# Rounding the first weight folds, keeping the conditions in PSUM and reordering the second norm in a two-layer backbone kernel

## The chip, the cores and the metric

The kernel runs on one core of a Trainium2 chip. The time is device microseconds of one execution. In profile rows PE is TensorE (matrix products), DVE VectorE, ACT ScalarE, POOL GpSimd, SP the queue that issues most DMAs. SBUF is the on-chip memory, PSUM the banks into which PE writes.

## The reference

Batch 1, 1024 latent tokens, 256 context tokens, width 1024, two layers. What matters here, cut from the code:

```python
shift, scale, gate = jnp.split(silu(c) @ mod_w[l] + mod_b[l], 3, axis=-1)
hx = modulate(rmsnorm(x, norm_g[l]), shift[:, None], scale[:, None])
# even layer: (and the same for the context tokens with silu(c_ctx))
z = h @ w_in                    # va, vg, ga, xb, gb
# conv branch from va, vg, ga; recurrent branch from xb, gb; then @ w_out
# odd layer:
z = h @ w_in; u, g = jnp.split(z, [2048], axis=-1)
d = multiscale_pool(u)          # four groups of 512 channels
y = jnp.einsum("bngi,gij->bngj", d, w_grp) * scale
out = (y * silu(g)) @ w_out
x = x + gate * out
```

## The kernel before

Nearly all products of the kernel run on numbers rounded for TensorE's quick float32 form. An operand is split in a high part (a cast on ACT) and a low part (source minus high part, on POOL or DVE), and a product is three matmuls: high by high, high by low, low by high. This is `split`. A plain float32 matmul needs no split but takes PE longer.

The odd layer's pooling is linear over tokens, so its group weights can be multiplied into its input weights beforehand. This is the fold: for each of four groups g and four steps kp, 128-row blocks of `wu[g, kp]` times `grp[g]`, two halves s, four chunks i, summed in PSUM, copied by ACT to an `fo` tile and stored to DRAM as `wfold[g]`. Much later the odd layer loads `wfold` as its weights (`wr_v`). In names like `fold_1_2_0` stand group, step and half.

The kernel has a first stage and then one long chain of products. In the first stage the inputs are loaded, the conditions silu(c) are spread over all partitions (`cL` for the latent tokens, `cC` for the context, in SBUF), and `modulation(k)` computes shift and scale as dots: DVE multiplies a 128x1024 tile `mod` with cL or cC and sums along the row (`junk`), then adds the bias (`m`, `a`, tiny instructions of 128x2). The squares of x are summed, PE adds them over partitions (`ms_x`), `rstd_cols` takes the root and spreads it; DVE scales x (`scaled` rows: `x<-x,a,ms_x`), and `h0h`, `h0l` are the high and low part of the modulated x. The folds of groups 0 and 1 run on PE beside this as plain float32 matmuls (`fold_whole`); `fold_some(n)` sets how many steps are written at a place. Then the first product, xb, begins.

The late stage is at the end of the even layer. `quad` computes one 2x2 block product with seven products of half-size operands (a, c, b are PSUM banks, `put` evicts them). The last `quad` of the output projection `woa` ends with products t3 and t4 into bank b. There the second norm follows: the squares of the new x1 are summed in `nacc` by ACT and DVE, PE's column matmuls (128x1) sum over partitions, ACT takes the root, DVE builds the diagonal `dg`, a matmul with ones spreads it (`ms_n`), and DVE scales x1. The folds of groups 2 and 3 run here, rounded (`fold`), to fill PE meanwhile. After them the odd layer's products start (qa_v).

Within an engine the instructions run in the order in which a scheduler put them, from the written order and priorities (`tc.high_priority`, `tc.issue_after`); across engines they wait by semaphores.

## Time and profile before

| | |
|---|---|
| runs | 1288.49, 1291.21, 1292.29 us; median 1291.21 |
| span of the profiled execution | 1287.8 us |
| PE busy | 1271.1 us (99%) |
| DVE busy | 1141.3 us (89%) |
| ACT busy | 640.6 us (50%) |
| POOL busy | 354.3 us (28%) |
| mean granted TensorE clock | 0.998 |

The time of the profiled execution itself is not given beside its span, which is 3.4 us less than the median of the runs. The busy shares are averages over stages: DVE, for instance, is busy 39.5 us of the 40 from 40 to 80 us, and 24.8 of the 40 from 740 to 780.

### The profile page before, as it was taken

The page shows a single profiled execution, that of the slowest core. Times are in us where ns is not written, and L with a number is a line of the kernel's source. Part 1 is how long each engine was busy: PE and PEld are TensorE (multiplying, and loading weights), DVE is VectorE, ACT ScalarE, POOL GpSimd, SP SyncE. Part 2 cuts the span into 40 slices and gives each one's busy share as a digit, 9 for nine tenths or more (in the row PEclk, how much of TensorE's full clock was granted, in tenths as well). Part 3 has the DMA queues.
Part 4 walks back from the last instruction along what each step waited for, and adds up shares of the span by engine and source line. Part 5 has one row for each costly group of instructions (what it writes and reads, how often), then busy time and mean ns, then how long its engine had stood idle before and what let it go on. Part 6 is the DMA issues. An engine that isn't in the chain of part 4 may idle for free.

```text
span 1287.8 us, 15841 instructions
## 1 busy us (share of the span) xinstructions
PE 1271.1 (99%) x5650; PEld 1027.5 (80%) x5650; DVE 1141.3 (89%) x1775; ACT 640.6 (50%) x941; POOL 354.3 (28%) x180
## 2 busy tenths in 40 slices
PE   8999999999999999999999999999999999999997
PEld 4468888888888888888887888888888888878886
DVE  7979999999999999988789667999999997887876
ACT  5343656666657623227426345834444444654543
POOL 3063655675558603443220023000000000000002
PEclk9999999999999999999999999999999999999999
DMA  9934111121212133543555356243333324777723
GB/s 371 358 114 157 58 41 63 44 74 42 66 41 90 50 115 107 168 147 113 172 174 192 127 185 203 87 155 127 110 132 131 123 96 157 245 247 258 296 83 131
DMA packets 83075, 181.87 MB, mean 141 GB/s; under 512 B 7858, under 2 KB 27826, under 8 KB 82996
## 3 DMA queue, kind: packets, MB, share of 16 engines
q1 hardware_dynamic: 74548, 176.67, 40.1%
q10 hardware_dynamic: 8448, 4.20, 1.1%
q8 instruction: 44, 0.72, 0.2%
q14 instruction: 35, 0.29, 0.1%
HBM read 136.79 MB, written 44.04 MB: 140 GB/s over the span
## 4 chain that ended last, share of the span: by engine, by line
PE 86%; DVE 6%; DMA 5%; ACT 1%; issue 1%; SPq 0%; POOL 0%; POOLq 0%; DVEq 0%; ACTq 0%
PE vg L510 7%; PE wob L510 7%; PE gb L510 7%; PE va L510 7%; PE xb L510 6%; PE g L510 4%; PE fold L285 3%; PE ga L510 2%; PE qb_v L1000 2%; PE qb_v L1001 2%; PE qb_v L998 2%; PE xbc L510 2%; PE qb_g L1000 2%; PE qb_g L1001 2%; PE qb_g L998 2%; DMA x<-xT 1%
## 5 line engine op out<-in xcount | busy, mean ns | idle before, releaser
L510 DVE SCALAR_TENSOR_TENSOR conv<-u,sm,conv 128x505 f32<-128x505 f32 (+6 forms) x224 | 153.9, 748 | 0.9
L1762 POOL TENSOR_TENSOR o<-x,rr 128x256 f32<-128x256 f32 (+1 forms) x10 | 9.4, 971 | 445.7 <-ACT rr L1698 443.8
L510 POOL TENSOR_TENSOR l<-l,l 128x1280 f32<-128x1280 f32 (+1 forms) x23 | 64.0, 2798 | 91.8 <-DVE l L510 65.5
L510 ACT ACTIVATE l<-g,sm 128x512 f32<-128x512 f32 (+1 forms) x96 | 58.7, 619 | 57.7 <-PE g L510 57.0
L285 PE MATMUL fold<-graw,wu 128*128 128x512 f32 x128 | 58.0, 614 | 2.3 <-DMA wu<-wu 2.3
L102 ACT CAST wq_g<-wr_g 128x512 fp32r<-128x512 f32 x48 | 28.3, 622 | 48.4 <-DVE wr_g L979 17.6
L285 PEld LDWEIGHTS fold<-graw,wu 128*128 128x128 f32 x128 | 25.1, 198 | 33.7 <-issue 32.7
L510 PE MATMUL vg<-h0h,wl_vg 128*128 128x512 f32 x128 | 50.0, 390 | 0.0
L510 PE MATMUL wob<-ybh,wh_wob 128*128 128x512 f32 x128 | 49.9, 390 | 0.0
L510 PE MATMUL vg<-h0h,wh_vg 128*128 128x512 f32 x128 | 49.8, 389 | 0.0
L510 PE MATMUL gb<-h0l,wh_gb 128*128 128x512 f32 x128 | 49.8, 389 | 0.0
L510 PE MATMUL gb<-h0h,wh_gb 128*128 128x512 f32 x128 | 49.8, 389 | 0.0
L510 PE MATMUL wob<-ybh,wl_wob 128*128 128x512 f32 x128 | 49.8, 389 | 0.0
L510 PE MATMUL vg<-h0l,wh_vg 128*128 128x512 f32 x128 | 49.8, 389 | 0.0
L510 PE MATMUL wob<-ybl,wh_wob 128*128 128x512 f32 x128 | 49.8, 389 | 0.0
L510 PE MATMUL va<-h0h,wh_va 128*128 128x512 f32 x128 | 49.8, 389 | 0.0
L510 PE MATMUL va<-h0l,wh_va 128*128 128x512 f32 x128 | 49.8, 389 | 0.0
L510 PE MATMUL va<-h0h,wl_va 128*128 128x512 f32 x128 | 49.8, 389 | 0.0
L510 PE MATMUL gb<-h0h,wl_gb 128*128 128x512 f32 x128 | 49.8, 389 | 0.0
L510 DVE TENSOR_TENSOR_SCAN l<-l,l 128x256 f32<-128x256 f32 (+1 forms) x32 | 48.7, 1521 | 1.1
L103 POOL TENSOR_TENSOR wl_wu<-wr_wu,wh_wu 128x1024 fp32r<-128x1024 f32 x8 | 19.2, 2417 | 106.9 <-ACT wh_wu L102 104.4
L510 POOL TENSOR_TENSOR l<-l,uc 128x1280 f32<-128x1280 f32 x16 | 48.1, 3032 | 0.0
(642 smaller groups left out, 4344.0 us busy)
## 6 DMA issues: line engine op xcount, KB each, us to landing
mod<-modT SPq DMA_DIRECT2D x20, 512.0 KB, 5.5
x_part<-xp SPq DMA_DIRECT2D x32, 256.0 KB, 3.1
mod<-modT SPq DMA_DIRECT2D x32, 256.0 KB, 3.1
wr_v<-wfold SPq DMA_DIRECT2D x16, 512.0 KB, 4.0
wr_g<-wg SPq DMA_DIRECT2D x16, 512.0 KB, 4.2
wr_wo<-wo SPq DMA_DIRECT2D x16, 512.0 KB, 4.6
y_b<-y SPq DMA_DIRECT2D x24, 256.0 KB, 3.4
y_t<-y SPq DMA_DIRECT2D x24, 256.0 KB, 2.9
```

Source lines behind the costliest of these rows:

```text
L102: return (nc.scalar.copy(hi, src), eng.tensor_tensor(out=lo, in0=src, in1=hi.bitcast(F32), op=sub))
L103: eng.tensor_tensor(out=lo, in0=src, in1=hi.bitcast(F32), op=sub))
L285: nc.tensor.matmul(ps, w[:, kc], gs[i], start=(i == 0), stop=(i == 3))
L510: last[eng] = f(*args, **kw)
L998: nc.tensor.matmul(ps, hi, xh[k], start=(first and k == 0), stop=False, skip_group_check=not first)
L1000: nc.tensor.matmul(ps, hi, xl[k], start=False, stop=False, skip_group_check=not first)
L1001: mm = nc.tensor.matmul(ps, lo, xh[k], start=False, stop=(k == KH - 1), skip_group_check=not first)
L1762: nc.gpsimd.tensor_tensor(out=outs[k // per][:, k % per], in0=x1[k][:, cols], in1=rr, op=mult)
```

## The change

Three things change.

1. `fold_whole` becomes `fold_early`. Only the very first step, (0,0), stays plain float32. The other steps of groups 0 and 1 are three rounded products, and two of the four steps of group 2 come into the first stage. The raw group weights and the weights of each step are split: casts on ACT, subtractions on POOL (one on DVE). Group 0's results are stored later (`fold_store`).
2. The conditions stay in PSUM, in two tiles `cps` of two banks each, and the dots read them there. `cL` is copied later, for its later readers. The modulation is divided into `load_mod` and `dots`, which are written apart. The roots of x (`x_roots`) use two of the four `pm` banks.
3. In the late stage fold2 has only steps 2 and 3. The last squares (x1_6's second half and x1_7's first) are not added by DVE but summed by PE with more column matmuls (`norm_cols`), and columns, roots and folds have a written order on PE: half 1 first, then half 0.

```diff
-        folds = (u for g in range(2) for u in fold_whole(g, fo_tile, g_tile, raw_tile))
+    EARLY = ((0, 1, 2, 3), (0, 1, 2, 3), (0, 1))
+        folds = (u for g in range(3) for u in fold_early(g, EARLY[g], fo_tile, g_pair(g)))
...
+    def fold_early(g, kps, out_tile, g_tile):
...
+            raw = (dtile if g < 2 else xtile)(f"graw_{g}_{i}")
             load(raw, grp[g, i])
+            th, tl = g_tile(i)
+            split(raw, th, tl, nc.gpsimd)
...
+            load(w, wu[g, kp])
+            if (g, kp) == (0, 0):
+                parts = ((w, gs),)
+            else:
+                wh, wl = [wpool.tile([P, D], F32R, tag=t, name=f"{t}_wu_{g}_{kp}") for t in ("wh", "wl")]
+                split(w, wh, wl, nc.vector if (g, kp) == (0, 1) else nc.gpsimd)
+                parts = ((wh, gh), (wh, gl), (wl, gh))
...
-        cC = spool.tile([P, D], F32, name="cC")
+        cps = [sp.tile([P, D], F32, name=f"c_{i}") for i in range(2)]
...
+                nc.vector.scalar_tensor_tensor(out=junk, in0=raw, scalar=1.0, in1=cps[i], op0=mult, op1=mult,
+                                               accum_out=m0[:, i, m : m + 1])
...
+        nc.scalar.copy(cL, cps[0])
...
+    def norm_cols(h, mm):
...
+        for c in range(H // P):
+            cs = slice(c * P, (c + 1) * P)
+            on("pe", nc.tensor.matmul, nps[h][0][:, c : c + 1], nacc[h][:, cs], ones[:, 0:1], start=True, stop=False)
+            on("pe", nc.tensor.matmul, nps[h][0][:, c : c + 1], q[:, cs], ones[:, 0:1], start=False, stop=True)
...
+                if m == LASTW and i != h:
+                    nsq[h] = ttile(f"n1q{m}_{i}_{h}")
+                    last["act"] = nc.scalar.activation(nsq[h], v, AF.Square)
+                else:
+                    square_acc(nacc[h][:, :H], v, (m, i) == (0, h), f"n1q{m}_{i}_{h}")
...
-    fold2 = fold(2, wr_tile, vtile, d2tile, [None, None, dtile, dtile])
+    fold2 = fold(2, d2tile, vtile, d2tile, [wring_tile] * 2, (2, 3))
...
-    rs = [rstd_cols(nacc[h][:, :H], f"n1{h}", idD, hpool, h, marks) for h in range(2)]
+    some(fold2, 6)
+    with tc.high_priority(offset=EVAC):
+        rs[1] = norm_root(1)
+        norm_cols(0, last["pe"])
+    some(fold2, 7)
+    with tc.high_priority(offset=EVAC):
+        rs[0] = norm_root(0)
```

The order on the engines shows the change at three places. First POOL in the first stage, from the last sum of x's squares (`ssq`) to the first weight of the product xb; `csq` are the squares of the context. Before:

```order
L340 TENSOR_TENSOR ssq_156<-ssq_156,xsq_0_327 128x512
L340 TENSOR_TENSOR ssqc<-ssqc,csq_1_547 128x256
L340 TENSOR_TENSOR ssqc<-ssqc,csq_2_550 128x256
L340 TENSOR_TENSOR ssqc<-ssqc,csq_3_553 128x256
L340 TENSOR_TENSOR ssqc<-ssqc,csq_0_575 128x256
```

After, the `ctl` rows being the low parts of group 1's raws:

```order
L361 TENSOR_TENSOR ssq_157<-ssq_157,xsq_0_403 128x512
L102 TENSOR_TENSOR ctl_138<-graw_0_482,cth_136 128x1024
L102 TENSOR_TENSOR ctl_139<-graw_1_486,cth_137 128x1024
L102 TENSOR_TENSOR wl_wu_0_495<-wu_0_492,wh_wu_0_494 128x1024
L102 TENSOR_TENSOR wl_wu_1_545<-wu_1_542,wh_wu_1_544 128x1024
L102 TENSOR_TENSOR wl_wu_2_599<-wu_2_596,wh_wu_2_598 128x1024
L102 TENSOR_TENSOR wl_wu_3_691<-wu_3_688,wh_wu_3_690 128x1024
L102 TENSOR_TENSOR gl_0_729<-graw_0_726,gh_0_728 128x1024
L102 TENSOR_TENSOR gl_1_735<-graw_1_732,gh_1_734 128x1024
L102 TENSOR_TENSOR wl_wu_0_741<-wu_0_738,wh_wu_0_740 128x1024
L361 TENSOR_TENSOR ssqc<-ssqc,csq_1_780 128x256
```

Nine subtractions stand between the two sums now, where nothing stood. DVE's order over the same time is nearly the old one; here is the changed kernel's piece around the scaled rows of x_292 (the fourth tile of x), with the dots' condition `c` in PSUM:

```order
L374 SCALAR_TENSOR_TENSOR junk,m_129<-mod_3_586,c_154 128x1024
L378 TENSOR_TENSOR m_129<-m_129,sm 128x2
L374 SCALAR_TENSOR_TENSOR junk,m_129<-mod_11_588,c_153 128x1024
L374 SCALAR_TENSOR_TENSOR junk,m_129<-mod_11_588,c_154 128x1024
L381 SCALAR_TENSOR_TENSOR a_130<-m_129,mb_190,sm 128x2
L374 SCALAR_TENSOR_TENSOR junk,m_129<-mod_5_636,c_153 128x1024
L416 SCALAR_TENSOR_TENSOR x_292<-x_292,a_130,ms_x_412 128x512
L416 SCALAR_TENSOR_TENSOR x_292<-x_292,a_130,ms_x_423 128x512
```

It has the same dots, tiny adds and scaled rows as before in almost the same order; only where the dots read the condition differs. Next PE at the end of the first stage, up to the product xb. Before:

```order
L190 MATMUL ms_c<-ssqc,ones 128x256
L285 MATMUL fold_3_0_636<-graw_0_425,wu_3_634 128x512 x2
L285 MATMUL fold_3_0_636<-graw_1_427,wu_3_634 128x512 x2
L285 MATMUL fold_3_1_644<-graw_0_425,wu_3_634 128x512 x2
L285 MATMUL fold_3_1_644<-graw_1_427,wu_3_634 128x512 x2
L133 MATMUL xb_680<-h0h_461,wh_xb_675 128x512
```

After, where `fold_1_0_811` is step 1 of group 2:

```order
L304 MATMUL fold_1_1_812<-gl_0_729,wh_wu_1_807 128x512 x2
L304 MATMUL fold_1_1_812<-gl_1_735,wh_wu_1_807 128x512 x2
L189 MATMUL ms_c<-ssqc,ones 128x256
L304 MATMUL fold_1_0_811<-gh_0_728,wl_wu_1_808 128x512 x2
L304 MATMUL fold_1_0_811<-gh_1_734,wl_wu_1_808 128x512 x2
L304 MATMUL fold_1_1_812<-gh_0_728,wl_wu_1_808 128x512 x2
L304 MATMUL fold_1_1_812<-gh_1_734,wl_wu_1_808 128x512 x2
L132 MATMUL xb_922<-h0h_582,wh_xb_917 128x512
```

Steps (2,0) and (2,1) now end the stage. Last, PE in the late stage, from the last product into bank b (qb_woa, t4) to the columns of the norm. Before, 22 folds stand ahead of t4, of which one is shown, and the columns follow it:

```order
L260 MATMUL fold_0_1_6174<-gh_1_6118,wh_wu_0_6124 128x512
L998 MATMUL qb_woa_5973<-ya_t4h_5503,wq_woa_4_5914 128x512
L1000 MATMUL qb_woa_5973<-ya_t4l_5505,wq_woa_4_5914 128x512
L1001 MATMUL qb_woa_5973<-ya_t4h_5503,wq_woa_4_5914 128x512
L998 MATMUL qb_woa_5973<-ya_t4h_5503,wq_woa_4_5914 128x512
```

After, six folds follow t4, then 8 columns of half 1, whose end is shown, its root and the columns of half 0:

```order
L567 MATMUL ms_n_6319<-ones,n1acc_5758 128x1
L567 MATMUL ms_n_6319<-ones,n1q_0_1_6308 128x1
L567 MATMUL ms_n_6319<-dg_n_6331,ones 128x512
L567 MATMUL ms_n_0_6386<-ones,n1acc_5757 128x1
L567 MATMUL ms_n_0_6386<-ones,n1q_1_0_6339 128x1
```

and seven folds later the root of half 0:

```order
L567 MATMUL fold_2_0_6378<-gh_1_6350,wl_wu_2_6357 128x512
L567 MATMUL fold_2_0_6378<-gh_1_6350,wh_wu_2_6356 128x512
L567 MATMUL fold_2_0_6378<-gl_1_6351,wh_wu_2_6356 128x512
L567 MATMUL fold_2_0_6378<-gh_1_6350,wl_wu_2_6357 128x512
L567 MATMUL fold_2_1_6410<-gh_0_6344,wh_wu_2_6356 128x512
L567 MATMUL ms_n_1_6387<-dg_n_6399,ones 128x512
L567 MATMUL fold_2_1_6410<-gl_0_6345,wh_wu_2_6356 128x512
```

No fold stands between the columns of half 1 and its root, and seven between the columns of half 0 and its root; before, at least 22 folds stood between each of them.

More of the change, by code (lines that the diff above doesn't have):

```diff
@@ L447, in ctx_split, with x_roots @@
                 modulate_ctx(k)
-        mb1 = spool.tile([P, KD], F32, name="mb1")
-        def first_weights():
-            fold_some(2)
-            load(sm, small)
-            nc.vector.tensor_scalar(out=mb1, in0=col(O_MB + KT, KD), scalar1=1.0, scalar2=None, op0=add)
-        modulation(0, first_weights)
+        def x_roots(h):
+            n = H // P
+            ps = psum(f"ms_x{h}")
+            r = spool.tile([P, n], F32, name=f"rc_x{h}")
+            for c in range(n):
+                nc.tensor.matmul(ps[:, c : c + 1], acc[h][:, c * P : (c + 1) * P], ones[:, 0:1], start=True, stop=True)
+            nc.scalar.activation(r, ps[:, :n], AF.Sqrt, bias=eps_r)
+            nc.vector.reciprocal(r, r)
+            t = ttile(f"dg_x{h}")
+            nc.vector.tensor_tensor(out=t.rearrange("p (c t) -> p c t", t=P),
+                                    in0=idx.unsqueeze(1).to_broadcast([P, n, P]),
+                                    in1=r.unsqueeze(2).to_broadcast([P, n, P]), op=mult)
+            nc.tensor.matmul(ps, ones, t, start=True, stop=True)
+            return ps
+        mb1 = spool.tile([P, KD], F32, name="mb1")
+        load_mod(0)
+        fold_some(2)
+        load(sm, small)
+        nc.vector.tensor_scalar(out=mb1, in0=col(O_MB + KT, KD), scalar1=1.0, scalar2=None, op0=add)
+        dots(0)
+        load_mod(KT)
+        dots(KT)
         x_load(0)
@@ L499, in body @@
             decay_rates()
-        fold_some(10)
         chain[0] = None
+    pc = ctx.enter_context(tc.tile_pool(name="pc", bufs=1, space=PSUM, reuse_waits="tile"))
     last = {}
@@ L992, in wquad, with prod @@
         return p1, p2, p3, p4, p5, p6, p7
-    def prod(ps, w, op, first, last):
+    def prod(ps, w, op, first, last, between=None):
         xh, xl = op
         for k in range(KH):
+            if between is not None and k == KH - 1:
+                between(mm)
             hi, lo = w[:, k * P : (k + 1) * P], w[:, H + k * P : H + (k + 1) * P]
@@ L1009, in body, with quad @@
     high = {}
-    def quad(w, name, ops, put, ahead=None, later=()):
+    def quad(w, name, ops, put, ahead=None, later=(), between=None):
         p1, p2, p3, p4, p5, p6, p7 = w
@@ L1040, in quad @@
             put(0, 1, c, 1)
-        prod(b, p4, ops["t4"], False, True)
+        last["end"] = prod(b, p4, ops["t4"], False, True, between)
         with tc.high_priority(offset=EVAC):
```

182 lines of the change are left out of this document (114 added, 68 removed).

## The prediction

> **What bounds the kernel now.** I read the busy shares first, then the chain that ended last, then busy time by stretches, then the timelines of the two places that change. In a timeline row stand start, duration, engine, line, operation, output and input, and a count.
>
> ```profile
> PE 1271.1 (99%) x5650; PEld 1027.5 (80%) x5650; DVE 1141.3 (89%) x1775; ACT 640.6 (50%) x941; POOL 354.3 (28%) x180
> PE 86%; DVE 6%; DMA 5%; ACT 1%; issue 1%; SPq 0%; POOL 0%; POOLq 0%; DVEq 0%; ACTq 0%
> ...
> 40.00:60.00 20.00, 19.49 (x59) 8.69 (x58) 19.59 (x36) 5.37 (x7) 0.00 (x0) 1.00 1.06 374
> 60.00:80.00 20.00, 20.00 (x49) 9.12 (x48) 19.93 (x24) 12.73 (x21) 11.77 (x8) 1.00 0.50 157
> 80.00:100.00 20.00, 20.00 (x98) 16.48 (x97) 12.19 (x33) 8.33 (x11) 12.74 (x12) 1.00 0.39 141
> 780.00:820.00 40.00, 40.00 (x174) 32.43 (x173) 35.36 (x56) 27.66 (x47) 9.94 (x6) 1.00 0.52 158
> ```
>
> TensorE (PE) is busy 99% of the span and nearly always carries the chain. So a matmul taken away late pays in full unless a new wait eats it, and a delay of PE early on is carried to the end. In the first stage there are two full engines: from 40 to 80 us VectorE (DVE) is as full as PE (19.59 and 19.93 of 20). GpSimd (POOL) does nothing from 40 to 60. This matters, because the change gives POOL work exactly there.
>
> **The late stage: what leaves.** The early stage takes two of the four kp steps of the third group's fold. One step is 2 halves x 4 chunks x 3 rounded products = 24 matmuls, so 48 leave.
>
> ```profile
> 762.69 0.39 PE L260 MATMUL fold<-gh,wh_wu 128*128 128x512 f32 x1
> ...
> 767.67 0.39 PE L998 MATMUL qb_woa<-ya_t4h,wq_woa 128*128 128x512 f32 x1
> 770.40 0.95 PE L202 MATMUL ms_n<-ones,n1acc 128*128 128x1 f32 x8
> 783.63 1.02 PE L211 MATMUL ms_n<-dg_n,ones 128*128 128x512 f32 x2
> 778.68 0.26 ACT L203 ACTIVATE rc_n<-ms_n,eps_r 128x4 f32<-128x4 f32 x1 [1.25 <-PE ms_n L202]
> 778.97 0.18 DVE L206 RECIPROCAL rc_n<-rc_n 128x4 f32<-128x4 f32 x1 [0.28 <-ACT rc_n L203]
> 779.19 1.29 DVE L208 TENSOR_TENSOR dg_n<-cH,rc_n 128x512 f32<-128x512 f32 x2
> 784.69 10.62 DVE L1398 SCALAR_TENSOR_TENSOR x<-x,a,ms_n 128x512 f32<-128x512 f32 x16 [4.21 <-PE ms_n L211]
> ```
>
> Between the first two rows lie 22 fold matmuls: (767.67 - 762.69)/22 = 0.227 us each, so 48 save 10.9 us. Against that:
> - Columns. A norm half has 8 column matmuls instead of 4, since the last squares are summed by PE. By the 0.95 us for 4 that is +1.9 us for both halves.
> - The last product. Before, the 22 folds stand ahead of t4; they cover the time in which DVE reads bank b out of PSUM. Now t4 follows t3 directly: one eviction (0.74 us, row below) and two hand-overs, +1.0 us.
> - First root. PE goes straight from the columns of half 1 to its root. Before, the sqrt starts at 778.68 on the columns' end, and dg of one half ends at 779.19 + 0.65 = 779.84: 1.2 us, with a hand-over on either side +1.5 us. Folds covered it.
> - Second root. DVE now has the 8 scaled rows of half 1 ahead of the dg of half 0: from the root's start 1.06 us (784.69 - 783.63) to the first scaled row, 8 x 0.664 = 5.3, reciprocal and dg 0.8, hop 0.15: 7.3 us. PE has only the root (0.9), 8 columns (1.6 to 1.9) and 7 folds (1.6) meanwhile: +3.2 us.
> - POOL beside that dg: the weight subtractions of group 3 start right after the second sqrt on ScalarE (ACT), and dg reads two SBUF tiles. By the next part it can wait for one of them, 0 to 2.4 us; I take half, 1.1, since nothing shows whether the second weight has landed.
>
> Sum: -10.9 + 1.9 + 1.0 + 1.5 + 3.2 + 1.1 = -2.2 us. Bounds: -9.0 with no wait, +1 if dg waits whole and the raw tile behind the x1 stores in SP's queue is 2 us late as well. DVE's chain that follows the roots ends earlier by more than PE's, so it isn't late next; the two squares that DVE no longer adds cost ACT nothing new.
>
> **The first stage on PE.** A float32 kp step is 16 records, four steps in the first row below.
>
> ```profile
> 46.20 27.73 PE L285 MATMUL fold<-graw,wu 128*128 128x512 f32 x64
> 74.21 7.03 PE L285 MATMUL fold<-graw,wu 128*128 128x512 f32 x16
> 80.67 0.80 PE L133 MATMUL xb<-h0h,wh_xb 128*128 128x512 f32 x1
> ```
>
> 27.73/4 = 6.9 us against 24 x 0.227 = 5.4 us rounded. Before: 8 x 6.9 = 55.2; now 6.9 + 9 x 5.4 = 55.8. PE's own work there is a wash (+0.6). What decides is who feeds it. The rounded form needs for each weight and raw tile an ACT cast and a subtraction, nearly all of them on POOL.
>
> **What the subtractions do to DVE.** The rows of both engines where they meet, in the first stage and later:
>
> ```profile
> 44.30 1.28 DVE L392 SCALAR_TENSOR_TENSOR h0l<-x,m,h0h 128x1024 fp32r<-128x1024 f32 x1
> 51.52 0.17 DVE L358 TENSOR_TENSOR m<-m,sm 128x2 f32<-128x2 f32 x1
> 53.05 1.22 DVE L353 SCALAR_TENSOR_TENSOR junk<-mod,cL 128x1024 f32<-128x1024 f32 x1
> 63.27 1.73 DVE L392 SCALAR_TENSOR_TENSOR h0l<-x,m,h0h 128x1024 fp32r<-128x1024 f32 x1
> 64.93 1.74 DVE L353 SCALAR_TENSOR_TENSOR junk<-mod,cL 128x1024 f32<-128x1024 f32 x1
> 66.61 0.67 DVE L358 TENSOR_TENSOR m<-m,sm 128x2 f32<-128x2 f32 x1
> 68.39 1.75 DVE L353 SCALAR_TENSOR_TENSOR junk<-mod,cC 128x1024 f32<-128x1024 f32 x1
> 70.18 0.56 DVE L355 SCALAR_TENSOR_TENSOR a<-m,mb,sm 128x2 f32<-128x2 f32 x1
> 70.77 4.04 DVE L388 SCALAR_TENSOR_TENSOR x<-x,a,ms_x 128x512 f32<-128x512 f32 x6
> ...
> 61.53 4.07 POOL L340 TENSOR_TENSOR ssqc<-ssqc,csq 128x256 f32<-128x256 f32 x3 [32.54 <-ACT csq L339]
> 65.76 5.77 POOL L340 TENSOR_TENSOR ssqc<-ssqc,csq 128x256 f32<-128x256 f32 x4 [0.17 <-ACT csq L339]
> 71.49 2.37 POOL L103 TENSOR_TENSOR wl_xb<-wr_xb,wh_xb 128x1024 fp32r<-128x1024 f32 x1
> ...
> 105.31 3.66 POOL L510 TENSOR_TENSOR ul<-uc,uh 128x1280 fp32r<-128x1280 f32 x1 [3.32 <-ACT uh L510]
> 108.92 3.38 POOL L510 TENSOR_TENSOR wl_xb<-wr_xb,wh_xb 128x1024 fp32r<-128x1024 f32 x1
> ...
> 106.07 3.98 DVE L510 SCALAR_TENSOR_TENSOR l<-l,cL 128x1024 f32<-128x1024 f32 x1
> 109.98 3.40 DVE L510 SCALAR_TENSOR_TENSOR l<-l,cL 128x1024 f32<-128x1024 f32 x1
> ...
> 157.28 5.89 POOL L510 TENSOR_TENSOR l<-l,l 128x1280 f32<-128x1280 f32 x2 [3.53 <-ACT l L510]
> 162.03 1.17 DVE L510 SCALAR_TENSOR_TENSOR edge_junk<-u,sm 128x8 f32<-128x8 f32 x1
> ...
> 762.76 4.76 POOL L103 TENSOR_TENSOR wl_wu<-wr_wu,wh_wu 128x1024 fp32r<-128x1024 f32 x2 [2.50 <-PE qb_woa L1001]
> 763.33 0.74 DVE L1343 SCALAR_TENSOR_TENSOR x<-qc_woa,m,x 128x512 f32<-128x512 f32 x1
> 765.31 3.55 DVE L1333 TENSOR_TENSOR n1acc<-n1acc,n1q 128x512 f32<-128x512 f32 x2 [1.24 <-ACT n1q L1332]
> ```
>
> A dot that takes 1.22 us alone takes 3.98 and 3.40 beside POOL, and it ends about 1.1 us after POOL's instruction does. The two adds at 765.31 end at 768.86, which is POOL's end (767.52) plus two adds of 0.67. The tiny 128x8 instruction at 162.03 ends with POOL's at 163.2. So a DVE instruction with two inputs in SBUF waits for the whole of a POOL instruction that runs. With one input in PSUM it doesn't: 763.33 kept 0.74, and the scaled rows from 70.77 kept 0.67 apiece over the subtraction at 71.49.
>
> [...]
>
> The conditions in PSUM free the 12 dots after the first scaled row: two of them were lengthened (64.93 and 68.39), a gain of 1.0 us. What is left with two SBUF inputs between the first scaled row and the last are 14 instructions: five h0l and nine small adds to m and a of 0.1 to 0.2 us. POOL's queue has there nine subtractions of 2.4 us (21 us) where before it had nothing until 61.53. I laid the queues of the four engines side by side in their written order, with the durations above and no two of these instructions at once. Laid out so, the kernel before has its last scaled row done at 76.2 us (it was 74.7). In the changed kernel seven of the 14 find a subtraction running: the a behind the first scaled rows 0.7 us, the two a of the mod_scale step 1.9 and 2.3 (a subtraction slips in between them), then a 2.3, m 2.0, h0l of x_3 2.1, m 2.3: 13.6 us. The waits that the same instructions have before are 0.45 + 0.5 + 0.4, with the two dots 2.4, so the last scaled row moves by 13.6 - 2.4 = +11.2 us. Bounds: 0, if each subtraction falls beside a dot or a scaled row, and 9 x 2.4 = 21.6.
>
> Behind the last scaled row PE still has work, since the two x roots sit in two of the four PSUM banks until then: half of step (2,0), step (2,1) and ms_c, 36 x 0.227 + 0.6 = 8.8 us, and 0.3 until the weight's cast comes, 9.1. Before, xb starts 80.67 - (70.77 + 4.04) = 5.9 us after it. That is +3.2. First stage: +11.2 + 3.2 = +14.4. The pair of a's is the place I trust least, as two instructions back to back may leave POOL no gap; I take half of its 2.3 off: **+13.2 us**. Bounds: -2.4 + 3.2 = +0.8 with no waits, +22.4 with all nine whole; I stay near the lay-out, since its queues are the written ones.
>
> What else moves there costs nothing as long as that wait stands. SP issues four more loads of 512 KB (two raws, two weights); they stand behind the loads of the last dots, in the stretch where the DMA share falls to 0.50, and xb's weight behind them is needed some 20 us later than it lands. Group 0's eight stores move behind the loads; nobody waits for them before the odd layer. ACT has 14 more casts of about 1 us and the copy of cL, at a half-used engine; but its order is fixed, and the copies that free PE's other two banks stand behind h0h of x_3, which waits for DVE. PE is idle there by 3 to 4 us or more, hidden by the same wait for the last scaled row; with DVE quick this is the next thing late, and inside rival 1's +3.2.
>
> The shift stays: PE is never idle between there and the late stage, and ctx's subtractions, later by as much, are needed later by as much.
>
> **Sum.** 1287.8 (profiled span) + 13.2 - 2.2 = 1298.8. The span stands 3.4 us under the median of the runs, 1291.2; so 1302.2 us.
>
> **Rivals.**
> 1. Little blocking. The subtractions run while DVE does dots and scaled rows, which read PSUM. For it: 28 of DVE's instructions there do. Against: DVE is full, so what it waits isn't made good. First stage +3.2 - 1.0 = +2.2, late -2.2: 1291.2, no change.
> 2. Faster, by the late stage alone. It needs rival 1's first stage and the root waits hidden: if dg of half 0 gets ahead on DVE, or ACT and DVE answer quicker than the rows say, late is -9.0 and the time 1291.2 + 2.2 - 9.0 = 1284.4. It decides from a blocked time under 3 us. Against it: the written order puts 8 scaled rows ahead of that dg.
> 3. The full lay-out and a late stage that gives all back: 1291.2 + 14.4 + 1 = 1306.6, or more with further whole waits.
>
> **Chances.** Forecast 0.55 (own range 1296 to 1307), rival 1 0.20, rival 2 0.19, rival 3 0.06. A difference under 0.3% (3.9 us) can't be told from none here. The range 1285 to 1307 leaves out the lower half of rival 2 and most of rival 3. Faster 0.20, same 0.20, slower 0.60: rival 1 is "same", rivals 2 and 3 their sides.
>
> **What will show it.** The m, a and h0l rows between 40 and 90 us: I expect several of 2 us and more, the dots all 1.2; the last scaled row at 83 to 88; xb's first matmul at 91 to 97; the second root of the late stage 3 us or more after the seventh fold. Wrong would be: small rows all under 0.3 us, or xb before 85.

## The result: 1303.6 us against 1291.75

The changed kernel takes 1303.61 us (median of 4 runs, 1301.04 to 1306.4); the kernel before took 1291.75 us beside it (1288.49 to 1294.48). The ratio is 1.0102, with an interval of 1.0073 to 1.013: 1% slower, by 11.9 us between the medians and 13.3 us between the spans of the profiled executions, where 1302.2 us was forecast. The sum of the prediction was right within 2 us, but one of its steps was wrong by 6 us and hidden by another that was too large, so that the sum came out this close was in part luck. The execution that was profiled took 1302.88 us, with a span of 1301.1.

The page of the changed kernel: busy shares, then the chain that ended last, by engine.

```profile
PE 1271.5 (98%) x5722; PEld 1044.4 (80%) x5722; DVE 1155.6 (89%) x1774; ACT 655.4 (50%) x958; POOL 383.7 (29%) x192
PE 78%; DVE 11%; DMA 5%; issue 2%; POOL 1%; ACT 1%; SPq 1%; POOLq 0%; ACTq 0%; DVEq 0%
```

PE is busy for as long as before (1271.1), in a span that is 13.3 us longer, so it waits for 13 us more; and its busy time holds stretches at a lower clock, in which the same matmuls take longer (one of 128x512 comes every 0.43 us at half clock, from 136.61, and every 0.23 us at the full one, from 135.31). The chain shows the waiting too, PE 86% to 78% and DVE 6% to 11%. Busy time by stretches (PE, PEld, DVE, ACT, POOL, then PE's granted clock, the DMA share, GB/s) shows where:

```profile
40.00:60.00 20.00, 17.62 (x76) 11.60 (x76) 19.87 (x27) 10.34 (x13) 13.11 (x5) 1.00 0.97 355
60.00:80.00 20.00, 15.30 (x55) 11.68 (x54) 19.79 (x29) 10.93 (x18) 12.02 (x7) 0.83 0.70 233
80.00:100.00 20.00, 19.76 (x87) 15.90 (x86) 13.10 (x10) 9.88 (x15) 16.61 (x13) 1.00 0.50 153
120.00:140.00 20.00, 16.20 (x76) 13.29 (x75) 19.86 (x29) 4.55 (x8) 9.22 (x3) 0.91 0.33 106
780.00:820.00 40.00, 37.53 (x165) 30.54 (x164) 32.71 (x47) 21.02 (x35) 11.04 (x5) 0.91 0.43 136
```

PE lost 2.4 and 4.7 us in the first two stretches, 3.8 in the fourth and 2.5 in the last, and in three of them the granted clock is below 1. Before, PE was busy for 19.49, 20, 20 and 40 us in the first three and the last of them, at 1.00. I follow one matmul at a time through both traces (start after less start before):

| PE reaches | before | after | shift |
|---|---|---|---|
| xb, the first product of the layer | 80.67 | 90.79 | +10.1 |
| g, its first matmuls | 119.55 | 130.15 | +10.6 |
| gb, behind the wait in g | | | +16.1 |
| qa_v, behind the third and fourth group's folds | 812.61 | 826.24 | +13.6 |
| end of the span | 1287.8 | 1301.1 | +13.3 |

So there are three parts: +10.1 in the first stage, some +6 at 135 us, and -2 to -3 late.

**First stage.** The rows of DVE that the prediction spoke of, then POOL's of the same time, then PE's waits:

```profile
41.01 1.41 DVE L416 SCALAR_TENSOR_TENSOR x<-x,a,ms_x 128x512 f32<-128x512 f32 x2
42.33 1.38 DVE L381 SCALAR_TENSOR_TENSOR a<-m,mb,sm 128x2 f32<-128x2 f32 x1
...
46.33 2.12 DVE L230 SCALAR_TENSOR_TENSOR a<-m,sm 128x2 f32<-128x2 f32 x2
...
56.84 2.36 DVE L381 SCALAR_TENSOR_TENSOR a<-m,mb,sm 128x2 f32<-128x2 f32 x1
61.63 0.16 DVE L378 TENSOR_TENSOR m<-m,sm 128x2 f32<-128x2 f32 x1
...
69.28 3.28 DVE L420 SCALAR_TENSOR_TENSOR h0l<-x,m,h0h 128x1024 fp32r<-128x1024 f32 x1
72.48 2.32 DVE L378 TENSOR_TENSOR m<-m,sm 128x2 f32<-128x2 f32 x1
...
78.57 4.04 DVE L416 SCALAR_TENSOR_TENSOR x<-x,a,ms_x 128x512 f32<-128x512 f32 x6
```

```profile
41.33 4.68 POOL L102 TENSOR_TENSOR ctl<-graw,cth 128x1024 fp32r<-128x1024 f32 x2 [8.40 <-ACT cth L101]
45.98 5.91 POOL L102 TENSOR_TENSOR wl_wu<-wu,wh_wu 128x1024 fp32r<-128x1024 f32 x2
56.50 2.68 POOL L102 TENSOR_TENSOR wl_wu<-wu,wh_wu 128x1024 fp32r<-128x1024 f32 x1 [4.61 <-ACT wh_wu L101]
...
69.10 2.38 POOL L102 TENSOR_TENSOR gl<-graw,gh 128x1024 fp32r<-128x1024 f32 x1 [2.33 <-DMA wu<-wu]
72.05 2.73 POOL L102 TENSOR_TENSOR wl_wu<-wu,wh_wu 128x1024 fp32r<-128x1024 f32 x1 [0.58 <-ACT wh_wu L101]
```

```profile
69.56 2.08 PE L304 MATMUL fold<-cth,wh_wu 128*128 128x512 f32 x4 [3.70 <-ACT fo L309]
78.75 1.19 PE L304 MATMUL fold<-gh,wh_wu 128*128 128x512 f32 x4 [1.00 <-ACT fo L309]
82.01 1.20 PE L304 MATMUL fold<-gh,wh_wu 128*128 128x512 f32 x4 [0.24 <-DVE x L416]
88.51 0.59 PE L189 MATMUL ms_c<-ssqc,ones 128*128 128x256 f32 x2
90.79 0.40 PE L132 MATMUL xb<-h0h,wh_xb 128*128 128x512 f32 x1
```

An instruction of two elements a partition takes 2.36 us: it starts beside POOL's subtraction at 56.50 and ends at 59.20, with it (59.18). So do those at 42.33 (1.38), 46.33 (a pair, 2.12) and 72.48, and the h0l at 69.28, which takes 1.28 alone. The waits are 1.2 + 1.9 + 2.1 + 2.0 + 2.2 = 9.4 us between the first scaled row (x<-x,a,ms_x) and the last. The last ends at 82.61, where it ended at 74.81 before. PE had waited 3.70 us at 69.56 for an eviction copy (fo), which stands on ACT behind an h0h that itself waited for DVE's scaled rows. At 82.01 it waits only 0.24 us, for the last but one of these rows, and it reaches xb 8.2 us after the last. So DVE's delay comes to PE on two ways, through ACT's order and through the last scaled rows, and they end nearly together.

This is one execution. Three others with the same first stage (the experiments on the late stage "second root later", "both roots covered" and "the old norm") have waits of 7.2 us there, the last scaled row ending at 80.83 to 81.06 and xb at 88.98 to 89.22, which is +8.3 to +8.6 in place of +10.1.

**At 135 us.** A wait that the kernel before did not have:

```profile
134.98 0.50 PE L567 MATMUL g<-uh,wh_gw 128*128 128x512 f32 x1 [3.61 <-DVE u L567]
```

u is made by DVE from the layer's products, but DVE comes to it late, since the chain of the context came late (ms_c on PE, its root `sq_c` on ACT, its reciprocal on DVE, the decay's small instructions). Two rows of DVE in the trace of the kernel before:

```profile
78.32 1.75 DVE L193 RECIPROCAL ssqc<-sq_c 128x256 f32<-128x256 f32 x1
...
119.18 1.28 DVE L510 TENSOR_TENSOR u<-va,sg 128x512 f32<-128x512 f32 x2
```

and the same two in that of the changed kernel:

```profile
93.33 1.75 DVE L192 RECIPROCAL ssqc<-sq_c 128x256 f32<-128x256 f32 x1 [4.49 <-ACT sq_c L191]
...
134.24 1.28 DVE L567 TENSOR_TENSOR u<-va,sg 128x512 f32<-128x512 f32 x2
```

Both moved by 15.0 us, where PE moved by 10.1. DVE is not what made the reciprocal late: its last h0l ends at 88.85, and it idles 4.49 us until the root comes. Two orders are behind it. On PE, ms_c now stands 8 matmuls ahead of xb, where it stood a whole float32 step (7.03 us) ahead; so it moved by 14.7 us (73.78 to 88.51). And on ACT the root, whose ms_c ends at 89.10, has the cast of vg's weight ahead of it, which waits for its load:

```profile
91.88 1.05 ACT L101 CAST wh_vg<-wr_vg 128x1024 fp32r<-128x1024 f32 x1 [4.68 <-DMA wr_vg<-win]
92.83 0.47 ACT L191 ACTIVATE sq_c<-ms_c,eps_r 128x256 f32<-128x256 f32 x1
```

In the kernel before, the root stood ahead of that cast (76.37 and 81.76). The load is issued at 87.79, right behind POOL's last subtraction for the fold (84.36 to 87.77), and lands at 91.78. Had the root followed ms_c at once, the reciprocal would have started some 3.7 us sooner (an estimate from these rows), which is the whole of the wait. Other runs agree: the three executions named above have the root 3.6 to 3.8 us behind ms_c and waits of 3.61 and 3.62 us at g; in "small adds with one tile in SBUF" below, the root comes 0.6 us behind ms_c, and the wait is 0.78 us. With the clock that is granted behind the wait (last section), the step from xb to gb is some 6 us.

**Late.** PE's three new waits:

```profile
779.64 0.50 PE L1057 MATMUL qb_woa<-ya_t4h,wq_woa 128*128 128x512 f32 x1 [1.11 <-DVE x L1425]
787.10 1.10 PE L567 MATMUL ms_n<-dg_n,ones 128*128 128x512 f32 x2 [1.38 <-DVE dg_n L567]
795.52 1.12 PE L567 MATMUL ms_n<-dg_n,ones 128*128 128x512 f32 x2 [1.08 <-DVE dg_n L567]
```

Between the two roots, 8 columns and 7 folds took 6.4 us, where they took 1.84 us (the columns of half 1) and 7 x 0.227 us at the full clock. That is 3.0 us more, at a granted clock that fell to half (rows in the last section).

### The profile page after: what moved, and what is told of

Its sections match the earlier page's. It is cut to its first block, busy times and chain, and to the rows that moved or that the text cites. A ratio compares the mean times of both kernels' runs of the same rounds, so it can differ in the third digit from the quotient of the medians.

```text
span 1301.1 us, 16034 instructions
## 1 busy us (share of the span) xinstructions
PE 1271.5 (98%) x5722; PEld 1044.4 (80%) x5722; DVE 1155.6 (89%) x1774; ACT 655.4 (50%) x958; POOL 383.7 (29%) x192
## 4 chain that ended last, share of the span: by engine, by line
PE 78%; DVE 11%; DMA 5%; issue 2%; POOL 1%; ACT 1%; SPq 1%; POOLq 0%; ACTq 0%; DVEq 0%
PE wob L567 7%; PE gb L567 7%; PE xb L567 6%; PE vg L567 6%; PE va L567 6%; PE g L567 4%; PE fold L567 2%; PE fold L304 2%; PE ga L567 2%; PE qb_v L1057 2%; PE qb_v L1059 2%; PE qb_v L1060 2%; PE qb_g L1057 1%; PE qb_g L1059 1%; PE qb_g L1060 1%
## 5 line engine op out<-in xcount | busy, mean ns | idle before, releaser
L567 DVE SCALAR_TENSOR_TENSOR conv<-cL,wsum,conv 128x506 f32<-128x506 f32 (+3 forms) x70 | 47.5, 745 | 0.2
L101 ACT CAST wq_wo<-wr_wo 128x512 fp32r<-128x512 f32 x48 | 28.8, 620 | 36.7 <-DMA wr_wo<-wo 13.0
L102 POOL TENSOR_TENSOR wl_wu<-wr_wu,wh_wu 128x1024 fp32r<-128x1024 f32 x6 | 14.8, 2469 | 105.0 <-ACT wh_wu L101 96.8
```

The costliest lines, as they stand in the source:

```text
L101: return (nc.scalar.copy(hi, src), eng.tensor_tensor(out=lo, in0=src, in1=hi.bitcast(F32), op=sub))
L102: eng.tensor_tensor(out=lo, in0=src, in1=hi.bitcast(F32), op=sub))
L567: last[eng] = f(*args, **kw)
```

## Experiments

All were timed beside the kernel before; ratios are to it, and differences in us are between medians, so where the two differ the ratio is the safer one. In three groups: what DVE waits for, the wait at 135 us, and the late stage. The changed kernel has the ratio 1.0102.

### What DVE waits for

**No subtractions.** In the early folds the low part is replaced by the high part, so that the matmuls and casts stay and the subtractions go (the raws' in the same way):

```diff
-                split(w, wh, wl, nc.vector if (g, kp) == (0, 1) else nc.gpsimd)
-                parts = ((wh, gh), (wh, gl), (wl, gh))
+                nc.scalar.copy(wh, w)
+                parts = ((wh, gh), (wh, gh), (wh, gh))
```

> Leaves out the low parts in the early folds: each of the three products is taken with the high parts, so PE's matmuls, the casts and the loads stay, but the subtractions of raws and weights (nine of 2.4 us on GpSimd between 40 and 90 us, one on DVE) are gone; the output lacks the low products. Theory 1 (DVE waits for GpSimd's subtractions): m, a and h0l rows before 77 us all under 0.3 and at most 1.4 us, last scaled row at 74 to 76, xb at 81 to 85, so 6 to 10 us less than the changed kernel; the context's squares end earlier as well, and the wait at 135 us shrinks from 3.6 to under 1.5 us: 1303.6 - 8 - 4 = about 1292. Theory 2 (PE waits for eviction copies that stand behind h0h on ScalarE, and for banks held by the roots): xb at 88 or later, time over 1299. A third, that more loads slow the stage: as theory 2, with the DMA share over 0.9 until 60 us as now.

Measured: 1293.69 us, ratio 1.0018 (1.0005 to 1.0032): 9.9 us less. The last scaled row ends at 74.03, xb starts at 82.37, the wait at 135 us is one of 1.52 at 124, and the first stage's small rows read like this one (the m at 66.07 takes 0.15):

```profile
54.56 0.22 DVE L381 SCALAR_TENSOR_TENSOR a<-m,mb,sm 128x2 f32<-128x2 f32 x1
```

Casts, matmuls, loads and eviction copies are as many as in the changed kernel. So it is the subtractions that cost the 10 us, and not the new form's copies, banks or loads. Of this, 8.4 us show at xb and the rest at g. Whether the subtractions cost it through DVE, or because PE itself waits for the low parts, this run doesn't tell; the adds on ScalarE, below, keep them.

**Small adds with one tile in SBUF.**

```diff
-                nc.vector.tensor_tensor(out=v, in0=v, in1=col(O_MB + m).to_broadcast([P, 2]), op=add)
+                nc.vector.tensor_scalar(out=v, in0=v, scalar1=col(O_MB + m), scalar2=None, op0=add)
...
-                nc.vector.scalar_tensor_tensor(out=a0[:, :, k], in0=m0[:, :, m], scalar=mb1[:, k : k + 1],
-                                               in1=col(O_NG + k).to_broadcast([P, 2]), op0=add, op1=mult)
+                nc.vector.tensor_scalar(out=a0[:, :, k], in0=m0[:, :, m], scalar1=mb1[:, k : k + 1],
+                                        scalar2=col(O_NG + k), op0=add, op1=mult)
```

> The small adds to m and a of the first stage become instructions with one tile in SBUF (the others come as per-partition scalars). Nothing else changes. If DVE's two-input instructions wait for the whole of a GpSimd instruction (theory 1), the rows of a at 28.74, 42.33, 46.33 and 56.84 and of m at 72.48, 1.4 to 2.4 us each, fall to 0.1 to 0.3 us; the h0l at 69.28 (3.28) stays. Between the first and the last scaled row that is 1.2 + 2.0 + 2.2 + 2.2 = 7.6 us, of which some is met again by the next h0l: last scaled row at 75 to 79 in place of 82.6, and since two h0l and the seven folds of the third group then bind, xb at 85 to 88 in place of 90.8; time 1303.6 less 3 to 6 us. If the stage is bound by the eviction copies and PSUM banks that PE waits for (theory 2), the rows fall but xb stays at 90 to 91 and the time within 1 us of 1303.6. If one input in SBUF waits as well, the rows stay at 1.4 to 2.4 us.

Measured: 1303.11 us, ratio 1.0103 (1.0086 to 1.012), no change. The third case came (and the pair of a's at 46.53 takes 2.18):

```profile
28.90 2.45 DVE L381 TENSOR_SCALAR a<-m,mb,sm 128x2 f32<-128x2 f32 x1
```

An instruction with one tile in SBUF waits as long (2.45 us here, 2.44 in the changed kernel at 28.74). "Two inputs in SBUF", as the prediction had it, is too narrow. Whether it is the tile that waits or the scalars, which lie in SBUF too, no run shows.

**Small adds on ScalarE.** The same adds, moved off DVE (mb1 is now multiplied by the gain beforehand):

```diff
+                nc.scalar.activation(v, v, AF.Identity, bias=col(O_MB + m))
...
+                nc.scalar.activation(a0[:, :, k], m0[:, :, m], AF.Identity, bias=mb1[:, k : k + 1],
+                                     scale=col(O_NG + k))
```

> The small adds to m and a of the first stage are done by ScalarE (an Identity with the bias and the scale as per-partition scalars) and not by DVE, whether with one or with two tiles in SBUF. Theory 1 (DVE waits whole for GpSimd's subtractions): of the waits between the first and the last scaled row, about 9.7 us, only the h0l at 69.28 keeps its 2 us, so DVE could end the last scaled row at 75 to 77 in place of 82.6. Then what the prediction called the next thing late binds, the eviction copies and casts in ScalarE's order, and the small adds now wait there: xb at 85 to 88 in place of 90.8, time 1303.6 less 3 to 7 us. Rival: ScalarE's order makes each small add as late as DVE's wait did (a cast or copy that waits stands ahead of it); last scaled row at 81 or later, time within 2 us of 1303.6.

Measured: 1294.21 us, ratio 1.0036 (1.0022 to 1.005): 9.4 us less, more than expected. The last scaled row ends at 77.09, while DVE still loses 3.7 us in four h0l of 2.1 to 2.3 us. xb starts at 86.36, 4.4 us sooner, or 2.6 to 2.9 us sooner than in the three other executions of the unchanged first stage. The other 5 us came at g, which I had not counted in. The last scaled row is 5.5 us sooner but the reciprocal 8.9 (84.45 in place of 93.33), since ACT's order now has the root ahead of the cast of vg's weight (83.94 and 87.92); so this part is owed to an order that came with the edit, and not to DVE's waits alone. The wait shrinks to

```profile
126.68 0.50 PE L568 MATMUL g<-uh,wh_gw 128*128 128x512 f32 x1 [0.58 <-DVE u L568]
```

What the prediction called the next thing late is now seen at 66.12 and 79.54:

```profile
66.12 1.19 PE L304 MATMUL fold<-cth,wh_wu 128*128 128x512 f32 x4 [1.83 <-ACT fo L309]
79.54 2.11 PE L304 MATMUL fold<-gh,wh_wu 128*128 128x512 f32 x8 [1.80 <-ACT wh_wu L101]
```

**Conditions back in SBUF.** The dots read copies of the two conditions in SBUF:

```diff
+        for t, u in zip((cL, cC), cps):
+            nc.scalar.copy(t, u)
...
-                nc.vector.scalar_tensor_tensor(out=junk, in0=raw, scalar=1.0, in1=cps[i], op0=mult, op1=mult,
+                nc.vector.scalar_tensor_tensor(out=junk, in0=raw, scalar=1.0, in1=dvec[i], op0=mult, op1=mult,
```

> Undoes the conditions in PSUM for the dots alone: the two conditions are copied to SBUF after the silu, and the dots read those copies, so each dot has two inputs in SBUF again, beside GpSimd's subtractions. Theory 1: the dots between 41 and 77 us, all 1.21 to 1.22 in the changed kernel, meet up to nine subtractions of 2.4 us; some 4 to 7 of the dots take 2 to 3.6 us, the last scaled row moves by +4 to +9 us, and the time is 1307 to 1313. [...]

Measured: 1313.97 us, ratio 1.0185 (1.0168 to 1.0202): 10.4 us more; the last scaled row ends at 92.81, 10.2 later. Two rows of the dots (junk is their output), one ahead of the first scaled row and one behind it:

```profile
10.23 3.05 DVE L374 SCALAR_TENSOR_TENSOR junk<-mod,cL 128x1024 f32<-128x1024 f32 x1 [0.23 <-ACT cL L464]
...
54.24 3.36 DVE L374 SCALAR_TENSOR_TENSOR junk<-mod,cL 128x1024 f32<-128x1024 f32 x1
```

The size is a little above the range, and the place is not where I had looked: five dots before 35 us lose 5.8 us, and the first scaled row starts 4.9 us later; between 41 and 92 us only three dots are long (3.36, 3.12, 1.74). The two copies on ACT are part of the edit, and the first dot starts 2.4 us later behind one of them, so not all of the 10.4 us need be the dots' waiting. Without its conditions in PSUM the change would have been 1.85% slower and not 1.0%.

### The wait at 135 us

**Context ahead.** The context's load, squares and root are written earlier:

```diff
-        fold_some(3)
-        fold_store()
         ctx_load(0)
         ctx_load(1)
+        fold_some(3)
+        fold_store()
         nc.scalar.copy(cL, cps[0])
         fold_store()
-        fold_some(1)
         ctx_scale()
+        fold_some(1)
```

> The context's load, squares and root are written three fold steps (the load) and one fold step (the root) earlier; nothing else changes. Theory: PE's wait for u at 134.98 (3.61 us) and the half clock behind it come from the context's chain, which was moved by 15 us (its reciprocal 78.32 to 93.33) while PE moved by 10. One fold step is 24 x 0.227 = 5.4 us, so ms_c comes at about 83, the reciprocal at about 88, the dots of the decay 5 us earlier, and the wait at 135 us goes: -3.6 for the wait and -2 for the clock, 1303.6 - 5.6 = 1298. The fold step itself only changes places with ms_c. Rival: the squares of the context then hold GpSimd for 6.7 us ahead of the third group's subtractions, PE waits for these at 70 to 85 us, and xb comes up to 4 us later than 90.8: time 1301 to 1306.

Measured: 1304.19 us, ratio 1.0103 (1.0088 to 1.0118), no change. Its trace has both the theory and the rival: the reciprocal starts at 88.60 in place of 93.33, and from 120 to 140 us PE has no wait,

```profile
120.00:140.00 20.00, 20.00 (x104) 17.15 (x103) 19.86 (x30) 4.88 (x9) 5.65 (x3) 1.00 0.21 73
```

so the wait did come from the context's chain (here, too, the root stands ahead of the cast of vg's weight). But PE waits 3.53 us at 81.49 for the scaled rows, with all 48 matmuls of the third group's two steps still to come, where the changed kernel has done 12 of them by then. xb starts at 91.84, and 12 of the fold's matmuls stand between its second and third matmul (92.30 to 95.02). The 5.6 us were moved, not saved. (The first stage of the unchanged order gives xb at 88.98 to 89.22 in three other executions below, so the loss there is 3 to 6 us.)

### The late stage

**Second root later.**

```diff
-    some(fold2, 7)
+    some(fold2, 31)
```

> Only the late stage: the root of half 0 is issued on PE after 37 of the fold's 48 matmuls, not after 13. Theory: the wait of 1.08 us at 795.52 goes, since 24 more matmuls (5.4 us) stand ahead of the root, and the wait of 1.38 us at 787.10 stays; the scaled rows of half 0 come 4 to 5 us later and nobody needs them before the fourth group's fold ends. PE's idle time there falls by 1.1 us, and if the lower granted clock from 787 to 795 follows the idle time, by 1 to 2 us more: 1303.6 - 1 to 3 us. Rival: the scaled rows that come later make the next stage wait by as much, 0 or up to +4 us.

Measured: 1303.58 us, ratio 1.0098 (1.0083 to 1.0113): no gain that can be told from none. The second wait is gone, as expected, and the clock still falls:

```profile
800.59 1.02 PE L567 MATMUL ms_n<-dg_n,ones 128*128 128x512 f32 x2
```

From 790 to 795 us it is 0.50, and a fold matmul comes every 0.43 us (791.74 to 795.15) in place of 0.227. In the changed kernel the same slow stretch filled time in which PE had to wait for dg anyway, so taking the wait away should free little while the clock is at half. In this execution t4 also waited 1.81 us in place of 1.11, and the clock was at half behind it for 3.4 us, ahead of everything that the edit moves; so the trace alone doesn't price the edit.

**Both roots covered.** Ten folds between the columns of half 1 and their root as well:

```diff
-    last["pe"] = last["end"]
-    some(fold2, 6)
+    cols_end, last["pe"] = last["pe"], last["end"]
+    some(fold2, 4)
+    with tc.issue_after(cols_end.ins):
+        some(fold2, 10)
...
-    some(fold2, 7)
+    some(fold2, 20)
```

> Only the late stage, in another order on PE: four of the fold's matmuls ahead of the columns of half 1, ten between these columns and their root, twenty between the columns of half 0 and their root. Theory: the two waits (1.38 and 1.08 us) go, and with them the stretch at half clock from 788 to 795, since it follows 3 us in which PE did only columns of one element and waited (784 to 787): that stretch cost 8 columns x 0.6 us... in all 3.4 us (5 us at 0.82, 5 at 0.50). Together -1.4 - 1.1 - 3.4 = -5.9: 1297.7. Rival: the clock falls anyway, as it did when only the second root was moved: then -1 to -2.5, 1301 to 1302.6. A second rival: the scaled rows that come later are waited for by the next stage, 0.

Measured: 1300.8 us, ratio 1.0081 (1.0061 to 1.0101): 2.8 us less, half of what was expected, and by itself not clear of noise, since this interval and the changed kernel's overlap. In the trace, PE goes from the last qa_woa product to qa_v in 50.1 us, in place of 53.5. The wait at the first root is gone and the clock stays at 1.00 from 775 to 800 us; but the second root waits longer than in the changed kernel:

```profile
788.38 4.73 POOL L102 TENSOR_TENSOR wl_wu<-wr_wu,wh_wu 128x1024 fp32r<-128x1024 f32 x2 [10.50 <-ACT wh_wu L101]
...
790.90 2.75 DVE L567 TENSOR_TENSOR dg_n<-cH,rc_n 128x512 f32<-128x512 f32 x1
...
793.71 1.13 PE L567 MATMUL ms_n<-dg_n,ones 128*128 128x512 f32 x2 [1.98 <-DVE dg_n L567]
```

The dg takes 2.75 us and not 0.69, and ends at 793.65 behind POOL's second subtraction: the same wait as in the first stage.

**The old norm.** The written order of the second norm is undone; the folds stay as changed:

```diff
-                if m == LASTW and i != h:
-                    nsq[h] = ttile(f"n1q{m}_{i}_{h}")
-                    last["act"] = nc.scalar.activation(nsq[h], v, AF.Square)
...
+    marks = []
+    rs = [rstd_cols(nacc[h][:, :H], f"n1{h}", idD, hpool, h, marks) for h in range(2)]
```

> Undoes the written order of the second norm's roots and nothing else: columns and roots of both halves as in the kernel before (4 columns a half, DVE adds the last squares), with one fold step (23 of its matmuls) ahead of the last product t4, one step between the columns of the two halves, and the roots among the fourth group's fold. The third group still has only two late steps. Theory: folds cover t4's eviction, the sqrt and the second dg again, so the waits of 1.11, 1.38 and 1.08 us, the 1.9 us of columns and the 3.4 us of half clock go: 1303.6 - 5 to 8.9 = 1295 to 1298.6, and the late stage is 10.9 us shorter than in the kernel before. Rival: with 48 matmuls fewer the two roots come too late for the fourth group's fold to cover (the roots stood 13 and 15 us behind t4 before), or the raw weights aren't there and PE waits ahead of t4: 0 to +3 us, 1303 to 1307.

Measured: 1305.3 us, ratio 1.0105 (1.0089 to 1.0121): no gain. Up to the end of the folds the theory is right: PE has no wait ahead of t4, and goes from the last qa_woa product to qa_v in 46.7 us, in place of 53.5, with 1.7 us of waits for the fold's weights in it. Then it loses all of that again, for a reason that neither the theory nor the rival had:

```profile
794.29 10.62 DVE L1488 SCALAR_TENSOR_TENSOR x<-x,a,ms_n 128x512 f32<-128x512 f32 x16 [1.08 <-PE ms_n L210]
...
829.49 0.63 PE L1057 MATMUL qb_v<-x_t2h,wq_v 128*128 128x512 f32 x1 [2.58 <-ACT x_t2h L1483]
```

Both roots come at 793, DVE begins its scaled rows at 794 and is full until 850 us, and PE, with 48 matmuls fewer ahead of qa_v, now catches up with it: seven waits of 5.0 us up to 850 us, and behind the longest of them the clock at half for 3.4 us. From qa_v to the end it takes 10.2 us more than the changed kernel; the rest of that is in smaller pieces which I have not taken apart. In the changed kernel the first half's scaled rows begin at 788.24, and PE has none of these waits. So the early root of half 1 is needed as soon as the fold steps leave; it only stood bare.

**No third group early.** All four steps of the third group's fold late, the rest as changed:

```diff
-    EARLY = ((0, 1, 2, 3), (0, 1, 2, 3), (0, 1))
+    EARLY = ((0, 1, 2, 3), (0, 1, 2, 3), ())
```

> Puts the two steps of the third group's fold back to the late stage (all four steps there), and leaves the rest. Theory 1: three subtractions (64.36, 69.10, 72.05) and 48 matmuls leave the first stage; the waits of the h0l at 69.28 and the m at 72.48 go (4.2 us), the last scaled row comes at 78 in place of 82.6 and xb at 82 to 84 in place of 90.8, and the wait at 135 us shrinks. The late stage gains 48 x 0.227 = 10.9 us of matmuls. In all -7 to -9, -1 to -4 and +10.9: 1301 to 1306, no more than 2 us from the changed kernel. If the early steps were free because PE had holes there, as the change supposes, it is slower by 8 to 11 us: 1312. If they cost more than they save, under 1300.

Measured: 1310.04 us, ratio 1.0164 (1.0137 to 1.0192), 6.4 us slower (8 by the ratios), where I had said no more than 2, and nearer to the 1312 of "free" early steps. The last scaled row ends at 79.08, as expected (78), and g starts 8.9 us sooner than in the changed kernel. The late stage takes it all back and more:

```profile
764.84 5.70 POOL L102 TENSOR_TENSOR wl_wu<-wr_wu,wh_wu 128x1024 fp32r<-128x1024 f32 x2 [4.72 <-ACT wh_wu L101]
...
768.26 2.83 DVE L1388 TENSOR_TENSOR n1acc<-n1acc,n1q 128x512 f32<-128x512 f32 x1
...
772.46 0.80 PE L1057 MATMUL qb_woa<-ya_t4h,wq_woa 128*128 128x512 f32 x1 [5.33 <-DVE x L1425]
```

Besides the 10.9 us of matmuls, t4 waits 5.33 us for the eviction of its bank, since DVE, ahead of that eviction, idles 2.92 us for ACT's cast of the raw group weights and then has two instructions that lose 2.6 us to POOL's weight subtractions. So the two steps are better early, by 6 us, even with what they do to DVE there.

### Together

**Adds on ScalarE with the old norm, and with covered roots.** The edits are those above, put together; the second has thirty folds ahead of the second root:

```diff
-    some(fold2, 20)
+    some(fold2, 30)
```

> The small adds on ScalarE and the second norm as in the kernel before, together. If both effects are as separate as their places (first stage: 1303.6 - 9.4 = 1294.2; late stage: -5 to -8.9), 1285 to 1289, faster than the kernel before (1290.1) by 0.1 to 0.4%. Rival: the late stage gains nothing, 1294.

> The small adds on ScalarE and the covered roots, with thirty in place of twenty matmuls between the columns of half 0 and their root, since the dg of half 0 took 2.75 us beside GpSimd's weight subtraction and the root waited 1.98 us for it. 1294.2 less 2.8 (what the covered roots gave) and up to 2 more: 1289 to 1291.5, within 0.15% of the kernel before. Rival: the clock falls to half there all the same, 1293 to 1294.

Measured: 1295.58 us, ratio 1.0036 (1.0022 to 1.0049), and 1290.69 us, ratio 0.9998 (0.9987 to 1.001). The first is the rival, as the old norm by itself gives nothing. The second is what its parts add up to: 13 us are found again, and the kernel is as fast as before. Against the adds on ScalarE alone (1.0036, 1.0022 to 1.005) the covered roots' gain is clear of noise here. Its second root waits for nothing, and PE's clock is 1.00 in all stretches from 120 to 145 and 765 to 825 us.

**The last waits.** On top of that, six folds between t3 and t4, and the decay's chain right behind the context's root (some_fold2 stands for the two loads and the six matmuls):

```diff
         prod(b, p7, ops["t3"], False, False)
...
+        some_fold2()
         prod(b, p4, ops["t4"], False, True, between)
...
-        with tc.issue_after(last_cast[0].ins):
+        with tc.issue_after(root.ins):
             decay_rates()
```

> The small adds on ScalarE, the covered roots, and two more: six of the fold's matmuls stand between the products t3 and t4 on PE, and the decay's small chain (ScalarE's exponential and 23 small DVE instructions) follows the context's root at once, where DVE is idle (9.6 us behind 88.5), and not the context's last cast. Theory: the two waits of PE that are left, 1.07 us for t4's eviction and 0.60 us for u at 126, go: 1290.7 - 1.7 = 1289, which is under the kernel before (1290.65) by 0.1%. Rival: evictions come as late as before behind DVE's other work, and PE's wait only moves by six matmuls: 1290.7.

Measured: 1289.66 us, ratio 1.0001 (0.9992 to 1.001). Both waits are gone from the trace (no wait of PE from 110 to 150 us, none at t4), and the time is the same as before all the same. The profiled execution starts xb at 87.36, 1.4 us later than in the run above; whether the edit did that isn't settled, since executions with an unchanged first stage differ as much (90.79 in the changed kernel, 89.22, 89.10 and 88.98 in three experiments that touch only the late stage). It is also the slowest execution of the 11 (1293.47), and has waits that the run above has not (0.79 us at 819.30, 1.04 at 1118.11), so its trace doesn't price the edit. None of these versions beats the kernel before.

## Why the prediction came out

- **DVE waits for the whole of a POOL instruction: right, and the cause.** Taking the subtractions away gives 9.9 us, taking the small adds off DVE 9.4; of these, 8.4 and 4.4 stand at xb, and the rest came at g, where ACT's order has a part. A two-element a took 2.36 us beside a subtraction, and 0.22 where there were none. "With two inputs in SBUF" was too narrow; the tensor_scalar form waits too (2.45 us). With an input in PSUM it doesn't: the dots are all 1.21 to 1.22 us, as forecast.
- **The lay-out: right in kind, too large.** It had seven waits of 13.6 us, of which I took 12.4; six instructions waited, 9.4 us (7.2 in three other executions). The pair of a's was not split by a subtraction (2.12 us for both, where 1.9 + 2.3 were laid out), and the m at 61.63 met none (0.16). With 0.7 us for a later start and 2.4 for the waits that the kernel before had there, the last scaled row moved by 7.8 us, not 10. It ended at 82.61, just under the 83 to 88 that I gave.
- **PE's work behind the last scaled row**: 8.2 us, forecast 9.1; +2.3 in place of +3.2. So the first stage is +10.1 (+8.3 to +8.6 in the three others) against +13.2, and xb at 90.79 is just under 91 to 97.
- **"Later by as much, are needed later by as much": wrong, the step that failed.** The context's ms_c stands on PE behind more of the last fold step, and its root on ACT behind the cast of vg's weight, whose load comes late; so the reciprocal moved by 15.0 us, 5 more than PE. I had let the shift be the same for all engines, and had not laid out what follows the last scaled row on ACT and in SP's queue; of the loads there I had followed xb's weight only. Price: 3.61 us of wait and the clock behind it, 6 us in all. It made up for the 3.1 that the first stage was too large, and more. That the two nearly cancel is luck.
- **The 3.4 us between span and median.** Of them, 1.6 were that one execution being quicker than its median: here the median stands 2.5 us above the profiled span. So the shift came out 2.3 us larger than forecast (13.3 against 11.0), and the time 1.4.
- **Late stage: -2.2 forecast, -2.0 measured** (+15.7 at the last qa_woa product, +13.6 at qa_v). By terms: t4's wait 1.0 forecast, 1.11 measured; columns 1.9 and 1.8; first root 1.5 and 1.38; second root with its blocked dg 4.3, and 1.08 of wait with 3.0 of half clock, 4.1; dg beside POOL 1.1, and 1.76 - 0.69 = 1.07. With -10.9 they make -2.5. From the first root to the second are 8.4 us, as forecast (7.3 + 1.1), so the slow clock cost little there: PE had to wait for DVE anyway. But "the second root 3 us or more after the seventh fold" was wrong in form, since folds and columns at half clock filled the time.
- **DVE's chain behind the roots is not late next: right, and by less than I thought.** With the roots at 793 it binds, as the old norm showed.
- **Rivals.** Rival 1 (little blocking) is what the kernel would be without subtractions: 1293.7. Rival 2 needs both repairs at once, and the two together reach 1290.7, not 1284: xb still starts 5.3 us later than before (PE's waits for casts and copies remain), and of the 7.8 us that are won up to qa_v, 2.6 are lost behind it.

## What to carry to other kernels

When a transfer of work gives GpSimd elementwise instructions beside a full VectorE, list VectorE's instructions by where their operands lie: each one that reads only SBUF, however tiny, may wait for a whole GpSimd instruction (a two-element a took 2.36 us here, and 0.22 without the subtractions), and moving two-element adds to ScalarE was worth 9 us here, about half of it through the order that this left on ScalarE. When a stage is delayed, lay out every engine past it, since the engines are not delayed by the same amount and the one that comes latest makes the next wait; look also for a small instruction whose engine has a cast that waits for a load ahead of it. And when work that covered a chain is taken away, put what is left of it between the links of that chain: the same folds in another order gave some 3.5 us on top of the adds.
